# Filler of an SSD tied to single chunk outputs, and four of its sixteen tiles moved behind it

## The chip, the cores and the metric

The kernel runs on one core of a Trainium2 chip. The time is the device time of one execution in microseconds; three executions of the kernel before gave 1428.99, 1430.89 and 1433.18, median 1430.89. A profiled execution took 1432.96, with 1431.1 from its first to its last instruction; all durations below are from that one. The engines are PE (matmuls), DVE, ACT and POOL (elementwise work), and SP (which issues most DMAs).

## The reference

Two layers over 1024 tokens of width 1024 in float32, batch 1. The change touches the first layer only:

```python
def _even_layer(x, w_in, conv_w, conv_b, a_log, dt_bias, d_skip, norm_g, sc_conv_w, w_out):
    proj = x @ w_in
    z, xbc, dt_raw, sc_bg, sc_cg, sc_h, sc_gate = _split(proj, EVEN_SIZES)
    xbc = jax.nn.silu(_depthwise_conv(xbc, conv_w, SSD_CONV_PAD) + conv_b)
    xs, bm, cm = _split(xbc, (SSD_INNER, SSD_GROUPS * SSD_STATE, SSD_GROUPS * SSD_STATE))
    y_a = _ssd_bidirectional(xs, bm, cm, dt_raw, a_log, dt_bias, d_skip)   # shapes left out
    y_a = _rms_norm(y_a * jax.nn.silu(z), norm_g)
    y_b = sc_bg * _depthwise_conv(sc_cg * sc_h, sc_conv_w, (1, 1)) * jax.nn.silu(sc_gate)
    return jnp.concatenate([y_a, y_b], axis=-1) @ w_out

def _ssd_chunked(x, dt, a, bm, cm):          # one direction; 8 chunks of 128 tokens
    ...
    cb = jnp.einsum('bclgn,bcsgn->bcgls', cq, bq)
    y_diag = jnp.einsum('bcgls,bcgrls,bcsgrp->bclgrp', cb, _segsum_exp(cs), xd)
    states = jnp.einsum('bclgn,bcgrl,bclgrp->bcgrpn', bq, decay_states, xd)
    _, h_in = lax.scan(step, h0, (states, chunk_tot))   # h * exp(tot) + st, chunk by chunk
    y_off = jnp.einsum('bclgn,bcgrpn,bcgrl->bclgrp', cq, h_in, jnp.exp(cs))
    return y_diag + y_off
```

There are 16 heads of 64 in 4 groups of 4 heads; a group shares B and C (128 states). Branch B (`y_b`, the short convolution) needs four projections of 1024 columns each (sc_bg, sc_cg, sc_h, sc_gate) and nothing of the SSD.

## The kernel before

Every float32 product is made of fp32r matmuls on a high and a low part (hi·hi, hi·lo, lo·hi; `mm3` and `mm6`, L416 to L428). The list of operations is written by `main_plan` (L78) and run in that order; the framework then places the instructions in each engine's order by a simulation of its own, in which an instruction that is ready early may move ahead of others. `tc.issue_after(i)` adds an order edge: what is issued under it is not placed ahead of instruction i. It is an order, not a wait.

The first layer goes in five stages.

1. The input is split and the gate z of group 0 and dt are made. Then four tiles of branch B (j = 0).
2. Eight pairs of projections for x, B and C of the SSD. A pair is two weight tiles multiplied by a scheme of seven products in place of eight (`op_sp`, L937): 7 x 4 x 3 = 84 matmuls of 512 columns. Two separate tiles take 2 x 48.
3. The SSD, group by group. For each of eight chunks, in the order C2: three transposes (`xps`), a decay-weighted x (`xd`, split on ACT into `xdh` and on POOL into `xdl`) and the state product (`sps`) (`op_p2`, `op_p2s`); from group 1 on also the 24 gate matmuls of that chunk (`zps`, `op_z`). Then the late state additions (`op_p2b`: `hm` on POOL, an addition on DVE). Then, in the order C3, the outputs (`op_p3f` and `op_p3b`, L795 to L845): C·B into `cbp` (L801); the decay tile E, loaded by DMA from `crow` into one of four buffers (L804), biased on ACT (L809), merged under a mask on DVE (L810, L811), through Exp on ACT (L813), times C·B on DVE (L818); the state part `yo` on PE (L831), and the diagonal part on PE (L836, `cbp<-ssd,E`; "yd" in the code), which is the last to read E. Then additions on POOL and DVE, the gate, and a square on ACT.
4. Pairs of seven products for what is left of branch B.
5. The output projection and the norm, and then the second layer.

**The filler.** Branch B's tiles j = 1 to J0 - 1, four of 48 matmuls each (`gps`), are cut into 8 steps of 6 matmuls (`op_fm`, L696) and queued. FX steps are taken at the SSD's start, F2[g] at each of a group's eight chunks in its first half, F3[g] at each of its eight outputs. `op_hold` (L692) sets the instruction to which filler is tied by an order edge: the group's last transpose while its outputs are listed, nothing in between, and group 3's last yd behind the SSD. Only the first step of a tile is under the edge (L701: `hold is not None and kk == 0`); its other seven move as the placement has them. What is left in the queue stands behind the SSD. The values are F2 = (2, 0, 0, 0), F3 = (3, 3, 2, 2), J0 = 5: 16 tiles, and six pairs (j = 5 to 7) behind.

Of the kernel before, what the change touches and what calls it, by code (L numbers as in the profile page):

```python
# [18 lines left out]
P = 128  # L19
# [7 lines left out]
HD = 64  # L27
# [33 lines left out]


BR_ORDER = (1, 2, 0, 3)
F2, F3, FB, FX = (2, 0, 0, 0), (3, 3, 2, 2), 0, 8
JF, J0 = 1, 5
C2 = (0, 7, 1, 6, 2, 5, 3, 4)
C3 = (3, 4, 0, 7, 1, 6, 2, 5)
E_AT = 5
# [9 lines left out]
def main_plan():  # L78
    ops = []
# [5 lines left out]
    def pull(n):  # L85
        for _ in range(min(n, len(queue))):
            ops.append(queue.pop(0))
# [34 lines left out]
    for g in range(G):  # L122
        ops.append(("z0", g))
        pull(FB)
        for i, c in enumerate(C2):
            ops.append(("p2", g, c))
            if g > 0:
                ops.append(("z", g, c))
            pull(F2[g])
            if i > 0:  # L130
                ops.append(("p2s", g, C2[i - 1]))
        ops.append(("p2s", g, C2[-1]))
        ops.append(("p2b", g))
        if g + 1 < G:
            ops.append(("xl", g + 1))
        ops.append(("hold", g))
        ops.append(("p3f", g, C3[0]))
        for i, c in enumerate(C3):
            if i + 1 < NB:
                ops.append(("p3f", g, C3[i + 1]))  # L140
            if g == G - 1 and i == 2:
                ops.append(("tp", 0))
            if g == G - 1 and i == NB - 1:
                ops.append(("tp", 1))
            pull(F3[g])
            ops.append(("p3b", g, c))
        ops.append(("hold", None if g + 1 < G else "end"))
# [358 lines left out]
def layer0_main(k):  # L506
    nc, tc, a = k.nc, k.tc, k.a
    V, A, GP, PE = nc.vector, nc.scalar, nc.gpsimd, nc.tensor
# [126 lines left out]
    groups = [dict() for _ in range(G)]  # L635
# [53 lines left out]
    live = {}  # L689
    hold = None  # L690

    def op_hold(g):  # L692
        nonlocal hold
        hold = None if g is None else groups[-1]["yd"] if g == "end" else groups[g]["xp"]

    def op_fm(key, kk):  # L696
# [125 lines left out]
    def op_p3b(g, c):  # L822
        st = groups[g]
        M, yd = st.pop(("f", c))
        g4 = slice(4 * g, 4 * g + 4)
        blk = slice(P * c, P * c + P)
        xt = st["xtm"][:, c, :]
        yo = k.pb.tile([P, 512], F32, name="yo", tag="pb")
        cols = h_cols(c)
        d = dirs(cols)  # L830
        PE.matmul(yo[:, cols], st["xfm"][3][:, blk], st["hin"][:, c, cols], start=True, stop=True)  # L831
        to = t2("to")
        tov, yov = (t.rearrange("p (d h e) -> p d h e", d=2, h=HPG)[:, d] for t in (to, yo))
        V.tensor_tensor(out=tov, in0=yov, in1=bc_last(ecs4[:, c, d, g4], HD), op=ALU.mult)
        for h in range(HPG):
            st["yd"] = PE.matmul(yd[:, HD * h:HD * h + HD], M[:, P * h:P * h + P], xt[:, HD * h:HD * h + HD], start=True, stop=True).ins  # L836
        ta = t1("ta")
        GP.tensor_tensor(out=view(ta, HPG), in0=view(xt, HPG), in1=bc_last(st.pop(("cd", c)), HD), op=ALU.mult)
        for q in range(d.start, d.stop):
            GP.tensor_tensor(out=ta, in0=to[:, 256 * q:256 * q + 256], in1=ta, op=ALU.add)  # L840
        V.tensor_tensor(out=ta, in0=yd, in1=ta, op=ALU.add)
        yg = tp.tile([P, 256], F32, name="yg", tag="yg", bufs=3)
        V.tensor_tensor(out=yg, in0=ta, in1=st["zs"][:, c, :], op=ALU.mult)
        A.activation(out=ta, in_=yg, func=AF.Square, accum_out=k.ssq[:, c, g:g + 1])
        A.dma_start(out=k.yad[c, :, 256 * g:256 * g + 256], in_=yg)  # L845
# [794 lines left out]
```

## Time and profile before

| | |
|---|---|
| median of three executions | 1430.89 us (1428.99 to 1433.18) |
| the profiled execution, its span | 1432.96 us, 1431.1 us |
| PE busy | 1392.4 us (97%) |
| DVE, ACT, POOL busy | 936.3 (65%), 692.3 (48%), 443.5 us (31%) |
| E load from issue to landing, median | 6.3 us, 32 loads of 512 KB |
| a 512-column matmul in the filler, mean | about 400 ns from start to modelled end; they overlap |

Busy is the time in which an engine has an instruction under way, whatever its clock; an engine with a high share can be slowed all the same, and a mean over the span mixes stages. Matmuls are pipelined, so what one costs is read from the distance of starts, not from its duration. The granted clock (PEclk) is the share of full speed, with two levels, 1.2 and 2.4 GHz. A name in brackets behind a row of the timeline is what the engine had waited for, and how long.

### The profile page before, as it was taken

How to read it: one execution, taken by the hardware profiler on the slowest of the kernel's cores; microseconds unless marked ns; L12 is line 12 of the kernel's file. 1: busy time of each engine (PE TensorE's matmuls, PEld its weight loads, DVE VectorE, ACT ScalarE, POOL GpSimd, SP SyncE). 2: the span in 40 equal slices, each digit the busy share in tenths (PEclk: the TensorE clock that was granted, in tenths of full speed). 3: DMA queues.
4: the chain of work that ended last, by engine and by line, in shares of the span. 5: the costliest groups of instructions: out<-in, count | busy, mean ns of one | idle time of the engine just before them, and what ended most of it. 6: DMA issues, size and time to landing. Idle time of an engine off the chain costs nothing.

```text
span 1431.1 us, 19645 instructions
## 1 busy us (share of the span) xinstructions
PE 1392.4 (97%) x7215; PEld 1182.2 (83%) x7215; DVE 936.3 (65%) x1596; ACT 692.3 (48%) x1350; POOL 443.5 (31%) x420
## 2 busy tenths in 40 slices
PE   8999999999999899999999999999999999999997
PEld 7878888778888786788888888898888888988886
DVE  5887886466666677666575533723326888888485
ACT  5354554555565655333344332522225788888410
POOL 0031220344444454133210340611410454546210
PEclk9999999999999997999999999999999999999999
DMA  8332236634463424423258445201100000001232
GB/s 254 122 102 103 103 113 232 171 100 136 126 170 100 137 82 109 134 74 103 74 177 264 132 153 197 89 23 53 41 27 1 1 1 1 2 30 60 89 118 89
DMA packets 55520, 146.40 MB, mean 102 GB/s; under 512 B 6264, under 2 KB 11648, under 8 KB 55296
## 3 DMA queue, kind: packets, MB, share of 16 engines
q1 hardware_dynamic: 50816, 140.95, 31.7%
q10 hardware_dynamic: 4608, 4.20, 0.8%
q8 instruction: 57, 0.93, 0.3%
q14 instruction: 39, 0.32, 0.1%
HBM read 118.78 MB, written 26.35 MB: 101 GB/s over the span
## 4 chain that ended last, share of the span: by engine, by line
PE 69%; DVE 6%; DMA 3%; ACT 2%; issue 1%; POOL 0%; ACTq 0%; DVEq 0%
PE sA L953 5%; PE ops L427 4%; PE ops L425 4%; PE ops L424 4%; PE tps L1462 3%; PE fps L417 3%; PE fps L418 3%; PE fps L419 3%; PE sps L417 2%; PE sD L953 2%; PE sps L418 2%; PE sps L419 2%; PE gps L424 2%; PE gps L425 2%; PE gps L427 2%; PE o1ps L427 2%
## 5 line engine op out<-in xcount | busy, mean ns | idle before, releaser
L424 PE MATMUL gps<-x,whi 128*128 128x512 f32 x320 | 127.7, 399 | 0.3 <-ACT bru L672 0.3
L425 PE MATMUL gps<-x,whi 128*128 128x512 f32 x320 | 127.9, 400 | 0.0
L499 DVE TENSOR_TENSOR wlo<-wraw,whi 128x1024 fp32r<-128x1024 f32 x54 | 71.1, 1317 | 61.0 <-ACT whi L498 60.9
L1448 POOL TENSOR_SCALAR pt<-pt,sm 128x1024 f32<-128x1024 f32 x64 | 73.1, 1142 | 114.1 <-DVE sm L1447 63.5
L498 ACT CAST whi<-wraw 128x1024 fp32r<-128x1024 f32 x54 | 56.7, 1051 | 95.5 <-PE ops L427 38.2
L427 PE MATMUL gps<-x,wlo 128*128 128x512 f32 x320 | 102.7, 399 | 0.0
L902 POOL TENSOR_TENSOR s3t<-sraw 128x512 f32<-128x512 f32 x14 | 22.6, 1614 | 229.7 <-DMA sraw<-in_wt_dram 158.7
L499 DVE TENSOR_TENSOR PT<-tps,PT 128x512 fp32r<-128x512 f32 x128 | 84.1, 681 | 12.8 <-ACT PT L498 12.4
L1442 DVE TENSOR_REDUCE nm<-sps 128x1 f32<-128x1024 f32 x64 | 77.8, 1216 | 9.3 <-PE sps L419 9.0
L1446 ACT ACTIVATE pt<-sps,nm 128x1024 f32<-128x1024 f32 x64 | 71.8, 1122 | 17.6 <-DVE nm L1443 13.3
L1056 POOL TENSOR_TENSOR rs<-rs,neghalf 128x1 f32<-128x1 f32 x16 | 12.9, 811 | 210.7 <-DVE nm L1091 143.0
L498 ACT CAST PT<-tps 128x512 fp32r<-128x512 f32 x128 | 69.8, 588 | 16.1 <-PE tps L1462 15.6
L417 PE MATMUL fps<-x1hi,whi 128*128 128x512 f32 x192 | 74.9, 390 | 0.0
L419 PE MATMUL fps<-x1hi,wlo 128*128 128x512 f32 x192 | 74.7, 389 | 0.0
L418 PE MATMUL fps<-x1lo,whi 128*128 128x512 f32 x192 | 74.7, 389 | 0.0
L427 PEld LDWEIGHTS gps<-x,wlo 128*128 128x128 f32 x320 | 60.4, 190 | 14.0 <-issue 1.4
L424 PEld LDWEIGHTS gps<-x,whi 128*128 128x128 f32 x320 | 60.9, 190 | 13.3 <-ACT bru L672 0.8
L425 PEld LDWEIGHTS gps<-x,whi 128*128 128x128 f32 x320 | 60.9, 190 | 12.6 <-issue 0.7
L1462 PE MATMUL tps<-consts,pt 128*128 128x128 f32 x512 | 70.2, 273 | 0.3 <-DVE PT L499 0.3
L499 POOL TENSOR_TENSOR xdl<-xd,xdh 128x512 fp32r<-128x512 f32 (+1 forms) x32 | 38.8, 1213 | 101.8 <-ACT xdh L498 98.2
L646 DVE SCALAR_TENSOR_TENSOR cacc<-u,vec,cacc 128x1023 f32<-128x1023 f32 (+1 forms) x48 | 65.8, 1383 | 3.3 <-ACT cacc L643 3.0
L1477 PE MATMUL yps<-PT,vv 128*128 128x256 f32 x256 | 65.7, 286 | 0.0
(377 smaller groups left out, 4199.9 us busy)
## 6 DMA issues: line engine op xcount, KB each, us to landing
wraw<-in_wt_dram SPq DMA_DIRECT2D x70, 512.0 KB, 4.2
E<-crow SPq DMA_DIRECT2D x32, 512.0 KB, 6.3
sraw<-in_wt_dram SPq DMA_DIRECT2D x28, 512.0 KB, 3.7
xtraw<-in_xT_dram SPq DMA_DIRECT2D x16, 512.0 KB, 4.1
xbd<-cacc SPq DMA_DIRECT2D x16, 512.0 KB, 2.6
ssd<-xbd SPq DMA_DIRECT2D x16, 512.0 KB, 5.2
ybd<-bra SPq DMA_DIRECT2D x16, 256.0 KB, 2.8
yad<-yg ACTq DMA_DIRECT2D x32, 128.0 KB, 4.0
```

What stands on the lines that cost most here:

```text
L417: nc.tensor.matmul(out, shi, mhi, start=start, stop=False)
L418: nc.tensor.matmul(out, shi, mlo, start=False, stop=False)
L419: nc.tensor.matmul(out, slo, mhi, start=False, stop=stop)
L424: nc.tensor.matmul(out, shi, mhi, start=start, stop=False)
L425: nc.tensor.matmul(out, shi, mlo, start=False, stop=False)
L427: nc.tensor.matmul(out, slo, mhi, start=False, stop=stop)
L498: cast = nc.scalar.copy(out=hi, in_=src)
L499: lo_eng.tensor_tensor(out=lo, in0=src, in1=hi.bitcast(F32), op=ALU.subtract)
L953: st["last"] = PE.matmul(ps, s_[:, kk, :], x_, start=fresh and kk == 0 and m == 0, stop=kk == 3 and m == 2, skip_group_check=True).ins
L1442: V.tensor_reduce(out=nm, in_=ps, axis=AX.X, op=ALU.max)
L1448: GP.tensor_scalar(out=pt, in0=pt, scalar1=sm, scalar2=1.0, op0=ALU.mult, op1=ALU.mult)
L1462: PE.transpose(out=ps[:, P * c:P * c + P], in_=pt[:, P * (4 * h + c):P * (4 * h + c) + P], identity=k.ident)
```

## The change

```diff
-F2, F3, FB, FX = (2, 0, 0, 0), (3, 3, 2, 2), 0, 8
-JF, J0 = 1, 5
+F2, F3, FB, FX = (1, 0, 0, 0), (1, 1, 2, 3), 0, 8
+JF, J0 = 1, 4
...
                 ops.append(("tp", 1))
+            if i > 1:
+                ops.append(("hold", g, C3[i - 2]))
             pull(F3[g])
             ops.append(("p3b", g, c))
...
-    def op_hold(g):
+    def op_hold(g, c=None):
         nonlocal hold
+        if c is not None:
+            hold = groups[g]["yd", c]
+            return
         hold = None if g is None else groups[-1]["yd"] if g == "end" else groups[g]["xp"]
...
         for h in range(HPG):
-            st["yd"] = PE.matmul(yd[:, HD * h:HD * h + HD], M[:, P * h:P * h + P], xt[:, HD * h:HD * h + HD], start=True, stop=True).ins
+            st["yd"] = st["yd", c] = PE.matmul(yd[:, HD * h:HD * h + HD], M[:, P * h:P * h + P], xt[:, HD * h:HD * h + HD], start=True, stop=True).ins
```

J0 = 4 leaves 12 tiles in the filler and makes eight pairs behind the SSD. At the third and every later output of a group, filler that starts a tile is tied to the yd two outputs back. Group by group the plan takes 8 + 8, 0, 0, 0 steps in the first halves and 8, 8, 16, 24 at the outputs, where it took 8 + 16, 0, 0, 0 and 24, 24, 16, 16. The changed kernel has five lines more: its helpers' lines are two further down than before, those of the outputs five.

PE's order at the first outputs of group 0 (`yo` the state part, `cbp<-...E` the diagonal part, E_ with a number one chunk's decay tile, `gps` filler), before:

```order
L424 MATMUL gps<-x_91,whi 128x512
L836 MATMUL cbp<-ssd_1886,E_2265 128x64 x4
L425 MATMUL gps<-x_91,whi 128x512
L836 MATMUL cbp<-ssd_1886,E_2284 128x64 x4
L831 MATMUL yo<-ssd_1885,ssd_1887 128x512
L424 MATMUL gps<-x_93,whi 128x512
L425 MATMUL gps<-x_93,whi 128x512
L427 MATMUL gps<-x_91,wlo 128x512
L427 MATMUL gps<-x_93,wlo 128x512
```

And now, with the third to the fifth output (`zps` is a gate product of group 1):

```order
L421 MATMUL zps<-whi,x_93 128x256
L841 MATMUL cbp<-ssd_1886,E_2208 128x64 x4
L841 MATMUL cbp<-ssd_1886,E_2227 128x64 x4
L836 MATMUL yo<-ssd_1885,ssd_1887 128x512
L841 MATMUL cbp<-ssd_1886,E_2276 128x64 x4
L806 MATMUL cbp<-ssd_1887 128x128
L836 MATMUL yo<-ssd_1885,ssd_1887 128x256
L806 MATMUL cbp<-ssd_1887 128x128
L841 MATMUL cbp<-ssd_1886,E_2318 128x64 x4
L836 MATMUL yo<-ssd_1885,ssd_1887 128x256
L806 MATMUL cbp<-ssd_1887 128x128
```

No filler stands among the outputs of group 0 any more, nor among those of group 1; 24 gate matmuls of group 1 moved ahead of the first output and 24 behind it.

ACT's order there (`dtx` marks the Exp, `ed` the bias step, `cbp<-consts` the mask, `ta,ssq` the square), before:

```order
L813 ACTIVATE E_2345<-E_2345,dtx 128x128 x4
L809 ACTIVATE E_2469<-E_2469,ed 128x128 x4
L844 ACTIVATE ta,ssq<-yg 128x256
L845 DMA yad<-yg 128x256
L809 ACTIVATE E_2522<-E_2522,ed 128x128 x4
L498 CAST whi<-wraw 128x1024
L672 COPY bru<-gps 128x1024
L844 ACTIVATE ta,ssq<-yg 128x256
L845 DMA yad<-yg 128x256
L810 COPY cbp<-consts 128x128 x2
L813 ACTIVATE E_2399<-E_2399,dtx 128x128 x4
```

And now:

```order
L818 ACTIVATE E_2227<-E_2227,dtx 128x128 x4
L815 COPY cbp<-consts 128x128
L818 ACTIVATE E_2276<-E_2276,dtx 128x128 x4
L814 ACTIVATE E_2359<-E_2359,ed 128x128 x4
L815 COPY cbp<-consts 128x128
L814 ACTIVATE E_2400<-E_2400,ed 128x128 x4
L818 ACTIVATE E_2318<-E_2318,dtx 128x128 x4
L814 ACTIVATE E_2442<-E_2442,ed 128x128
```

Both times the Exp of the fourth chunk (E_2399, now E_2318) stands behind the bias step of the sixth (E_2522, now E_2400), whose buffer is the second chunk's; the weight cast, the filler's copy and the squares that stood between are gone from there.

PE's order at the last outputs of group 3, before:

```order
L801 MATMUL cbp<-ssd_1886 128x128
L831 MATMUL yo<-ssd_1885,ssd_1886 128x512
L836 MATMUL cbp<-ssd_1886,E_5008 128x64 x4
L801 MATMUL cbp<-ssd_1886 128x128
L831 MATMUL yo<-ssd_1885,ssd_1886 128x512
L836 MATMUL cbp<-ssd_1886,E_5068 128x64 x4
L836 MATMUL cbp<-ssd_1886,E_5125 128x64 x4
```

And now:

```order
L429 MATMUL gps<-x_93,wlo 128x512
L426 MATMUL gps<-x_91,whi 128x512
L427 MATMUL gps<-x_91,whi 128x512
L841 MATMUL cbp<-ssd_1886,E_4902 128x64
L806 MATMUL cbp<-ssd_1886 128x128
L841 MATMUL cbp<-ssd_1886,E_4902 128x64 x3
L836 MATMUL yo<-ssd_1885,ssd_1886 128x512
L426 MATMUL gps<-x_93,whi 128x512
L427 MATMUL gps<-x_93,whi 128x512
L429 MATMUL gps<-x_91,wlo 128x512
L429 MATMUL gps<-x_93,wlo 128x512
L836 MATMUL yo<-ssd_1885,ssd_1886 128x512
```

There the last five outputs stood without filler; now filler stands between outputs up to the last one.

## Rows read from the trace of the kernel before

**Rows 1.** The page: busy time, share of the span, instructions of each engine.
```profile
PE 1392.4 (97%) x7215; PEld 1182.2 (83%) x7215; DVE 936.3 (65%) x1596; ACT 692.3 (48%) x1350; POOL 443.5 (31%) x420
```

**Rows 2.** Busy time by stage: stretch, length, PE, PEld, DVE, ACT, POOL, PEclk, DMA share, GB/s.
```profile
246.50:299.50 53.00, 50.30 (x222) 40.66 (x221) 28.12 (x49) 27.71 (x69) 17.45 (x18) 0.94 0.53 149
266.00:279.00 13.00, 10.63 (x51) 8.26 (x50) 7.86 (x16) 8.34 (x24) 8.42 (x8) 0.86 0.63 147
299.50:337.20 37.70, 36.59 (x204) 29.54 (x203) 28.26 (x61) 19.81 (x61) 17.20 (x24) 1.00 0.60 164
337.20:377.80 40.60, 39.15 (x261) 35.53 (x260) 23.63 (x56) 24.81 (x74) 21.04 (x25) 1.00 0.33 99
377.80:415.40 37.60, 37.60 (x205) 30.86 (x204) 25.83 (x58) 20.45 (x63) 17.23 (x23) 1.00 0.66 168
415.40:455.80 40.40, 40.40 (x278) 37.30 (x277) 22.40 (x51) 24.66 (x72) 19.43 (x23) 1.00 0.36 106
455.80:490.50 34.70, 31.46 (x176) 25.33 (x176) 27.43 (x61) 18.74 (x61) 14.09 (x20) 0.95 0.50 143
490.50:529.50 39.00, 38.53 (x260) 35.17 (x259) 25.55 (x52) 26.83 (x75) 19.07 (x19) 1.00 0.26 80
529.50:567.00 37.50, 34.11 (x136) 25.29 (x135) 29.81 (x67) 19.38 (x62) 21.65 (x26) 0.75 0.45 116
544.00:567.00 23.00, 19.61 (x63) 13.57 (x63) 16.30 (x43) 14.95 (x49) 10.40 (x15) 0.60 0.26 80
592.20:735.00 142.80, 142.72 (x654) 118.15 (x655) 92.18 (x97) 50.85 (x66) 42.45 (x29) 0.99 0.29 94
```

**Rows 3.** Timeline of PE (start, duration, instruction) in filler; gate matmuls alone by stage.
```profile
286.51 0.39 PE L424 MATMUL gps<-x,whi 128*128 128x512 f32 x1
...
287.88 0.39 PE L424 MATMUL gps<-x,whi 128*128 128x512 f32 x1
...
474.60:477.70 3.10, 3.10 (x26) 3.10 (x26) 0.00 (x0) 0.00 (x0) 1.00 0.68 199
```

**Rows 4.** Timeline of ACT at the start of group 0.
```profile
257.51 1.01 ACT L672 COPY bru<-gps 128x1024 f32<-128x1024 f32 x1 [4.71 <-DMA xbd<-cacc]
...
261.06 0.39 ACT L498 CAST xdh<-xd 128x256 fp32r<-128x256 f32 x1
```

**Rows 5.** Timeline of PE at the first outputs of group 0.
```profile
299.53 1.02 PE L831 MATMUL yo<-ssd,ssd 128*128 128x512 f32 x2
...
303.11 1.00 PE L836 MATMUL cbp<-ssd,E 128*128 128x64 f32 x8
```

**Rows 6.** Timeline of ACT at the fourth to sixth chunk of group 0.
```profile
312.24 0.40 ACT L809 ACTIVATE E<-E,ed 128x128 f32<-128x128 f32 x1 [1.35 <-DMA E<-crow]
...
316.75 2.45 ACT L813 ACTIVATE E<-E,dtx 128x128 f32<-128x128 f32 x8 [0.61 <-DVE E L811]
```

**Rows 7.** Timeline of PE from group 2's fourth output to group 3's first transpose.
```profile
473.54 1.00 PE L836 MATMUL cbp<-ssd,E 128*128 128x64 f32 x8
...
490.45 0.49 PE L742 MATMUL xps<-consts,ssd 128*128 128x128 f32 x3
```

**Rows 8.** Timeline of ACT in the same stretch: the last chunk's bias step.
```profile
481.75 1.28 ACT L809 ACTIVATE E<-E,ed 128x128 f32<-128x128 f32 x4 [2.29 <-DMA E<-crow]
```

**Rows 9.** The page: DMA issues by line, number, KB each, median us to landing.
```profile
E<-crow SPq DMA_DIRECT2D x32, 512.0 KB, 6.3
```

**Rows 10.** The tile E in group 0 (290 to 345 us).
```profile
DMA to landing us min/median/max: 4.9/5.8/8.0
```

**Rows 11.** Timeline of PE at the end of group 3: two of its outputs' state parts.
```profile
543.10 0.70 PE L831 MATMUL yo<-ssd,ssd 128*128 128x256 f32 x2
...
563.31 2.02 PE L831 MATMUL yo<-ssd,ssd 128*128 128x512 f32 x2
```

**Rows 12.** Timeline of PE at the first outputs of group 1.
```profile
377.75 1.02 PE L831 MATMUL yo<-ssd,ssd 128*128 128x512 f32 x2
...
378.82 1.90 PE L836 MATMUL cbp<-ssd,E 128*128 128x64 f32 x16
```

## The prediction

> **What bounds the kernel now.** I read the page's busy shares first: PE is busy for 97% of the span [rows 1], so at first sight each matmul taken out is time gained. I then read busy time by stage, because a share over the whole span hides stages with another limit. There [rows 2] PE is full in the pairs behind the SSD (142.7 of 142.8 us), but in the SSD (246.5 to 567.0) it is idle for 12.4 us: 2.7, 1.1, 1.5, 0, 0, 3.2, 0.5 and 3.4 in its eight stretches, two for each group of heads (state products, then outputs). Its granted clock is 0.94, 0.95 and 0.75 in three of them; the engine ran at 1.2 in place of 2.4 GHz for a part of each, and 0.06 of 53.0, 0.05 of 34.7 and 0.25 of 37.5 us are 3.2, 1.7 and 9.4 us of work not done. So the filler hides the SSD's waits nearly everywhere, except at the end of group 3, where it ran out. Third I read what PE waits for where filler is thin: the E tiles (four buffers, eight chunks to a group). The buffer is free once a chunk's output product has read it, and must come back by DMA, pass ACT twice and DVE twice, before the chunk four further on can be multiplied.
>
> **The change part by part.** A 512-column matmul starts every 0.228 us: six from 286.51 to 287.88 [rows 3]. A filler tile is 48 of them, 11.0 us; a pair of seven products is 84, 19.2 us. The change takes four tiles out of the filler (192 matmuls, 43.8 us of PE) and puts two pairs behind the SSD (168, 38.4 us). The region of the pairs is full already, with DVE at 92 of 143 us and POOL at 42 [rows 2], which hides the pairs' weight splits and evictions, so the two pairs cost their **+38.4 us** in full. Everything then hangs on how much of the 43.8 us the SSD gives back. I counted the filler matmuls in the programs' order of PE:
>
> Group 0: 240 before (169 ahead of its first output, 71 among the outputs); 96 after, all ahead. Group 1: 144 before (55 and 89); 48 after, all ahead. Group 2: 54 and 42; 48 and 48 after. Group 3: 54 and 42; 48 and 96 after. Behind the last output, 144 both times: no change there.
>
> *Group 0, up to the first output* (53.0 us). ACT is held until 257.51 by the store of the last pair's result, whose memory the SSD's pools take over, and the first xdh comes at 261.06 [rows 4]. The change touches neither, so no state product starts before 261.5; the 48 filler matmuls that stand ahead of it fit in front, PE then waits. From there the order has six chunks with no filler between them. POOL was busy for 8.4 us over four such chunks in 266 to 279 [rows 2], 2.1 each: 12.6 us. Then come 48 filler matmuls (11.0), the last products (1.5) and 24 gate matmuls of group 1 that are now ahead of the first output; 26 of them took 3.1 us [rows 3], so 2.9 in all. That ends at 289.5, with about 1 for the last state additions at 290.5 against 299.5: **-9.0**. Bounds: with nothing to wait for after 261.5 (8 us of own products, 11.0, 2.9) 283.4, which is -16.1; at the whole 3.25 us per chunk which those four took, 296, -3.5. I take the value by POOL, since it is the engine whose work a chunk can't do without.
>
> *Group 0, the outputs* (37.7 us before), now with no filler. From the first yo to the end of the second chunk's yd it was 4.6 us (299.53 to 304.11), seven filler matmuls (1.6) among them [rows 5]; the 24 gate matmuls that stand there now make it 5.9. On ACT, the Exp of the fourth chunk stands behind the bias step of the sixth, which waits for the E tile that the second chunk's yd releases. From that release to the bias step it took 8.1 us (304.11 to 312.24) [rows 5, 6]; E loads took 4.9, 5.8 (median) and 8.0 in this group, 6.3 over all [rows 9, 10]. With 6.6 (the 6.3 and an issue), 1.28 for the bias step, half of 2.45 for the Exp and 1.7 for the product with C.B and the yd, the fourth yd ends 10.8 us later. It releases the buffer of the eighth chunk, and the row for this second turn is in group 2, whose end is bare already: fourth yd over at 474.54, bias step at 481.75, next group's first transpose at 490.45 [rows 7, 8], 15.9 us, or 15.3 with a 6.6 us load. Sum: 5.9 + 10.8 + 15.3 = 32.0, **-5.7**. With loads of 4.9 (5.2 with the issue) 29.2, -8.5; with 8.1 both times 35.0, -2.7. I take the median over all, because weight loads still stand on the same queue, though fewer.
>
> The Trainium skill (DMA: Bandwidth & Descriptors, Anatomy of one DMA) gives a transfer 2.0 us fixed and its bytes at 436 GB/s; for 512 KB I estimate 3.2 us by that, and by it each of the four turns here and in group 1 would be 3.1 us shorter, the whole change would come to -1.2 us, 1429.7, which is no change. The trace disagrees: the shortest of these E loads took 4.9 us [rows 10], and the sum stays with the rows.
>
> *Group 1.* Seven filler matmuls fewer ahead of the first output: **-1.6**, PE being full there but for 1.5 us. The outputs took 37.6 us. The first yo to the end of the second yd is 3.0 us (377.75 to 380.72) [rows 12], with nothing between them now as before; 3.0 + 10.8 + 15.3 = 29.1, **-8.5**; with the short and the long loads 26.3 and 32.1, -11.3 and -5.5. The 48 gate matmuls (5.8 us) lie inside the first turn.
>
> *Group 2.* Six matmuls move from the front to the outputs, -1.4 and +1.4. Its filler now begins behind the third output and lasts to the end, where PE idled for 3.2 us and lost 1.7 to the clock; being bare at its start instead, I take **-1** (-3 to +1).
>
> *Group 3.* In front -1.4. Among the outputs 54 more filler matmuls, 12.3 us, where PE lost 3.4 idle and 9.4 to the clock: 12.8. They fit: **-1.4** in all (-2.4 to +2.6).
>
> The SSD gives back 9.0 + 5.7 + 1.6 + 8.5 + 1 + 1.4 = 27.2 us of the 43.8; 38.4 - 27.2 = **+11.2**. The profiled execution took 1432.96 (its span is 1431.1), so 1444.2; it lies 2.1 above the median of the three runs shown, 1430.89, on whose scale this is **1442**.
>
> **The rivals.**
> *Faster: PE alone decides.* Place: the outputs of groups 0 and 1 and the front of group 0. If every E load takes the 4.9 us and the front of group 0 packs without a wait, all low ends together are 16.1 + 8.5 + 1.6 + 11.3 + 3 + 2.4 = 42.9, and the time changes by 38.4 - 42.9 = -4.5: 1426. It decides only once the SSD gives back over 42.7, that is, at these ends and nowhere short of them. For it speaks the 97% of rows 1; against it that this share counts a PE at half clock as busy, and that ACT sat waiting for E with filler still around it [rows 6, 8].
> The Trainium skill (Perfetto Trace Analysis, Identifying Performance Opportunities) has the most-contended engine set the gain. By that rule the 24 matmuls fewer would be 5.5 us less, 1425.
>
> *Slower still: both bare stretches at half clock.* At the end of group 3, when the filler was gone, PE was granted 0.60 of its clock over 23 us [rows 2], and from 543.10 to 563.31 five further chunks took 20.2 us, 4.05 each [rows 11]. Eight chunks at that pace and the start make 35.3 for group 0 and 33 for group 1, -2.4 and -4.6; with the front at -3.5 and the other terms as above the SSD gives 14.5, net +23.9: 1455. For it: a chunk's own products are 2.0 us of PE (1.07 from 377.75 to 378.82, and half of 1.90 [rows 12]) in a chunk of some 3.7. Against: group 2's bare end came back to full clock at once (0.95 over the stretch). The Trainium skill (TensorE: Matmul & The Clock Gate, HAM oscillation) says that bursts of matmuls with waits between them fall back to the lower clock over and over; by that rule it is this 1455.
>
> *No change.* Fewer weight loads share the queue with E, the loads fall to 4.9 and POOL's pace in the front to less than 2: 1.4 off each of four turns, 4 more in the front, net about +1: 1432.
>
> *The edges do nothing.* An edge sits on the first step of a tile only, and it orders, it does not wait. In groups 0 and 1 no tile starts among the outputs, so there it is without effect; in groups 2 and 3 the order shows the filler spread. Without it group 3 would end bare as before, about 10 us more; that is decided by the order already, and gets no chance of its own.
>
> **How the numbers follow.** 0.3% of the time is 4.3 us, about what can be told from no change. The forecast, +4.3 to about +20, has 0.60; both stretches at half clock 0.12; no change 0.17; PE alone 0.11. So slower 0.72, same 0.17, faster 0.11. The range is -3 to +25 around the median, 1428 to 1456: the low end leaves out only the last two microseconds of the low bounds, the high one some of the sum of the high bounds (-3.5, -2.7, -1.6, -5.5, +1, +2.6: 9.7 given back, +28.7).
>
> **What would show it.** Right: eight pairs dense behind the SSD, 38 us longer; group 0's outputs near 32 us and group 1's near 29 with PE well under nine tenths busy and a clock under 1; ACT waiting for E loads, and PE for the E product, far beyond before; group 3's outputs still about 37.5 us but at full clock; the first output of group 0 some 9 us earlier. Wrong: outputs of groups 0 and 1 in 26 us or less with PE full, which is the faster rival; E turns that take the rows' time while the SSD still gives back over 40, which would mean that my chain through ACT is not the one that binds; or a wait in the pairs' region, which I cost at none.

## The result and the profile after

The changed kernel takes 1451.77 us (median of four executions, 1448.48 to 1452.64), the kernel before 1432.04 (four executions, 1428.99 to 1433.65). The ratio is 1.0131, 95% interval [1.011, 1.0152]: slower, by 19.7 us. The forecast was 1442, its range 1428 to 1456. All readings below are from the profiled execution, which took 1452.45.

The busy shares on the page of the kernel after, beside [rows 1]:

```profile
PE 1391.2 (96%) x7191; PEld 1179.2 (81%) x7191; DVE 947.4 (65%) x1608; ACT 697.4 (48%) x1359; POOL 449.8 (31%) x427
```

PE has 24 matmuls and 1.2 us of busy time less, yet the span is 19.6 us longer. The page's total hides it; the stages show it. Busy time by stage after, in the columns of [rows 2]: front and outputs of groups 0 to 3, and the pairs behind the SSD:

```profile
250.50:293.70 43.20, 37.58 (x173) 30.32 (x172) 22.53 (x42) 24.50 (x62) 14.83 (x17) 0.88 0.58 163
293.70:328.10 34.40, 24.28 (x110) 17.25 (x109) 23.23 (x59) 17.59 (x63) 15.83 (x23) 0.77 0.55 139
328.10:366.10 38.00, 37.86 (x253) 34.69 (x252) 23.15 (x53) 23.51 (x72) 19.07 (x23) 0.98 0.38 111
366.10:399.60 33.50, 24.78 (x134) 18.97 (x134) 22.28 (x54) 18.24 (x61) 16.04 (x22) 0.82 0.75 148
399.60:437.90 38.30, 37.94 (x253) 34.84 (x252) 22.96 (x52) 23.35 (x72) 18.82 (x24) 0.98 0.39 119
437.90:470.00 32.10, 31.12 (x181) 25.28 (x181) 24.68 (x56) 20.50 (x63) 12.95 (x19) 1.00 0.67 154
470.00:510.00 40.00, 37.68 (x254) 34.19 (x253) 26.34 (x55) 24.76 (x71) 21.52 (x21) 1.00 0.28 76
510.00:549.20 39.20, 37.65 (x190) 29.54 (x189) 32.82 (x71) 21.68 (x68) 21.59 (x26) 1.00 0.45 127
574.70:755.00 180.30, 180.30 (x819) 149.31 (x820) 114.42 (x119) 63.35 (x84) 55.91 (x38) 0.99 0.28 89
```

The outputs of groups 0 and 1 (second and fourth line) are the new hole: PE is busy for 24.28 of 34.4 us and 24.78 of 33.5, at a granted clock of 0.77 and 0.82. The pairs are full to the last tenth. By stage, in us:

| stage | before | forecast | after |
|---|---|---|---|
| start to the first transpose | 246.5 | 246.5 | 250.6 |
| group 0, front | 53.0 | 44.0 | 43.2 |
| group 0, outputs | 37.7 | 32.0 | 34.4 |
| group 1, front | 40.5 | 38.9 | 38.0 |
| group 1, outputs | 37.6 | 29.1 | 33.4 |
| group 2, both | 75.1 | 74.1 | 70.5 |
| group 3, both | 76.5 | 75.1 | 79.2 |
| pairs, with the transposes for the projection among them | 142.5 | 180.9 | 180.4 |

The SSD gave back 320.4 - 298.7 = 21.7 us where the forecast had 27.2. Why the outputs are long is read from the timeline of ACT in the kernel after, group 0 (L814 is the bias step, L818 the Exp; brackets: waited for, and how long):

```profile
298.24 1.28 ACT L818 ACTIVATE E<-E,dtx 128x128 f32<-128x128 f32 x4 [2.94 <-DVE E L816]
304.03 1.28 ACT L814 ACTIVATE E<-E,ed 128x128 f32<-128x128 f32 x4 [4.51 <-DMA E<-crow]
305.21 0.25 ACT L815 COPY cbp<-consts 128x128 f32<-128x128 f32 x1
307.14 1.29 ACT L814 ACTIVATE E<-E,ed 128x128 f32<-128x128 f32 x4 [1.68 <-DMA E<-crow]
308.34 1.26 ACT L818 ACTIVATE E<-E,dtx 128x128 f32<-128x128 f32 x4
...
317.90 0.69 ACT L814 ACTIVATE E<-E,ed 128x128 f32<-128x128 f32 x2 [3.36 <-DMA E<-crow]
...
319.08 1.26 ACT L818 ACTIVATE E<-E,dtx 128x128 f32<-128x128 f32 x4
```

In ACT's order these are the Exp of the third chunk, the bias step of the fifth, the mask copy of the fourth, the bias step of the sixth, the Exp of the fourth, the bias step of the eighth, and the Exp of the sixth. The fourth chunk's Exp needs nothing that the sixth has, but stands behind it, and the sixth waits for its load. In the same way the sixth's Exp stands behind the eighth's bias step. PE in the same stretch (L836 yo, L841 the diagonal product, L747 the next group's transposes):

```profile
293.74 1.02 PE L836 MATMUL yo<-ssd,ssd 128*128 128x512 f32 x2
...
297.70 1.89 PE L841 MATMUL cbp<-ssd,E 128*128 128x64 f32 x16
...
306.79 1.22 PE L836 MATMUL yo<-ssd,ssd 128*128 128x256 f32 x2 [4.37 <-DVE ta L846]
...
310.38 1.97 PE L841 MATMUL cbp<-ssd,E 128*128 128x64 f32 x8 [1.94 <-DVE E L823]
...
328.15 0.85 PE L747 MATMUL xps<-consts,ssd 128*128 128x128 f32 x3
```

The second chunk's product ends at 299.59, the fourth's at 312.35, the next group begins at 328.15: a start of 5.85 us, a first turn of 12.76, a second of 15.80. The 4.37 us at 306.79 are put down to DVE, since yo waits for a PSUM tile that DVE has to read; DVE's own timeline shows what it was held by:

```profile
305.50 0.72 DVE L816 COPY_PREDICATED E<-cbp,E 128x512 f32<-128x512 int32 x1 [3.91 <-ACT cbp L815]
```

This is the merge of the fourth chunk. It waited for ACT's mask copy (L815), which stands behind the bias step at 304.03. So this wait leads through ACT to the E load as well, but to the fifth chunk's: the merge ended at 306.22, and of the fourth Exp's delay the sixth chunk's bias step added the 2.1 us from there to 308.34. On the page of the kernel after the loads have hardly changed from [rows 9]:

```profile
E<-crow SPq DMA_DIRECT2D x32, 512.0 KB, 6.1
```

### The profile page after: what moved, and what is told of

Read it like the earlier page. It is cut to its first block, busy times and chain, and to the rows that moved or that the text cites. A ratio compares the mean times of both kernels' runs of the same rounds, so it can differ in the third digit from the quotient of the medians.

```text
span 1450.7 us, 19639 instructions
## 1 busy us (share of the span) xinstructions
PE 1391.2 (96%) x7191; PEld 1179.2 (81%) x7191; DVE 947.4 (65%) x1608; ACT 697.4 (48%) x1359; POOL 449.8 (31%) x427
## 4 chain that ended last, share of the span: by engine, by line
PE 81%; DVE 8%; DMA 6%; ACT 2%; issue 2%; POOL 1%; SPq 0%; DVEq 0%; ACTq 0%; POOLq 0%
PE sA L958 12%; PE sD L958 6%; PE ops L427 4%; PE ops L429 4%; PE ops L426 4%; PE tps L1467 3%; PE fps L421 3%; PE fps L419 3%; PE fps L420 3%; PE sB L958 3%; PE sps L419 2%; DMA E<-crow 2%; PE sps L420 2%; PE sps L421 2%; PE o1ps L427 2%; PE o1ps L429 2%
## 5 line engine op out<-in xcount | busy, mean ns | idle before, releaser
L501 DVE TENSOR_TENSOR wlo<-wraw,whi 128x1024 fp32r<-128x1024 f32 x50 | 66.9, 1338 | 56.3 <-ACT whi L500 56.2
L426 PE MATMUL gps<-x,whi 128*128 128x512 f32 x256 | 101.4, 396 | 0.0
L427 PE MATMUL gps<-x,whi 128*128 128x512 f32 x256 | 101.3, 396 | 0.0
L500 ACT CAST whi<-wraw 128x1024 fp32r<-128x1024 f32 x50 | 52.5, 1050 | 97.1 <-PE ops L429 41.6
L429 PE MATMUL gps<-x,wlo 128*128 128x512 f32 x256 | 80.8, 393 | 0.0
L500 ACT CAST whi<-sraw 128x1024 fp32r<-128x1024 f32 x40 | 41.4, 1051 | 69.4 <-PE sD L958 39.9
L1467 PEld LDWEIGHTS tps<-consts,pt 128*128 128x128 f32 x512 | 59.7, 141 | 7.2 <-DVE PT L501 1.2
L958 PE MATMUL sA<-x,whi 128*128 128x512 f32 x192 | 60.5, 396 | 3.5 <-ACT whi L500 3.5
```

The costliest lines, as they stand in the source:

```text
L426: nc.tensor.matmul(out, shi, mhi, start=start, stop=False)
L427: nc.tensor.matmul(out, shi, mlo, start=False, stop=False)
L429: nc.tensor.matmul(out, slo, mhi, start=False, stop=stop)
L500: cast = nc.scalar.copy(out=hi, in_=src)
L501: lo_eng.tensor_tensor(out=lo, in0=src, in1=hi.bitcast(F32), op=ALU.subtract)
L958: st["last"] = PE.matmul(ps, s_[:, kk, :], x_, start=fresh and kk == 0 and m == 0, stop=kk == 3 and m == 2, skip_group_check=True).ins
```

## The experiments

Theory 1 was the forecast's mechanism: what bounds bare outputs is the E tile's way back through ACT's order. Against it stood the clock, the work of DVE and POOL, and the edges as such. The kernel before was timed beside each set: 1433.55 for the first four, 1432.88 for the next four, 1432.25 for the three after and 1429.89 for the last.

**The edges alone.** The changed kernel with the old numbers:

```diff
-F2, F3, FB, FX = (1, 0, 0, 0), (1, 1, 2, 3), 0, 8
-JF, J0 = 1, 4
+F2, F3, FB, FX = (2, 0, 0, 0), (3, 3, 2, 2), 0, 8
+JF, J0 = 1, 5
```

> The changed kernel with the numbers of the kernel before (F2 = (2,0,0,0), F3 = (3,3,2,2), J0 = 5): 16 filler tiles, six pairs behind the SSD, and the new order edges. Theory 1 (bare outputs are held by the E tile's turn through ACT; what filler stands late in a group hides it): the filler of groups 2 and 3 now reaches to their last outputs, where the kernel before lost 3.2 + 1.7 and 3.4 + 9.4 us idle or at half clock; some of the 17.7 comes back late in the group and some is lost at its bare start: 1425 us (1419 to 1431), group 3's outputs at 30 to 35 us in place of 37.5 with a clock of 0.9 or more. Rival (the edges decide nothing, only the number of tiles does): 1432, the same as before, within 3 us.

Measured: 1446.3 us, ratio 1.0096 [1.0079, 1.0112]. Both expectations missed: with the old numbers the edges cost 13 us. Group 0's outputs took 48.4 us in place of 37.7 (front 46.4 in place of 53.0), group 3's 43.3 in place of 37.5. In sum group 0 lost 4.1 us (not traced) and group 3 5.2. Group 3's outputs by stage, rows of ACT there in the kernel before, and then of ACT, PE and DVE in this kernel:

```profile
535.40:578.70 43.30, 32.90 (x142) 24.70 (x141) 29.64 (x70) 22.27 (x69) 20.86 (x26) 0.76 0.39 101
```

```profile
536.24 1.28 ACT L813 ACTIVATE E<-E,dtx 128x128 f32<-128x128 f32 x4 [1.39 <-DVE E L811]
...
540.51 1.28 ACT L809 ACTIVATE E<-E,ed 128x128 f32<-128x128 f32 x4 [3.00 <-DMA E<-crow]
```

```profile
549.82 0.98 ACT L814 ACTIVATE E<-E,ed 128x128 f32<-128x128 f32 x3 [3.36 <-DMA E<-crow]
...
551.00 1.26 ACT L818 ACTIVATE E<-E,dtx 128x128 f32<-128x128 f32 x4
```

```profile
553.04 1.97 PE L841 MATMUL cbp<-ssd,E 128*128 128x64 f32 x8 [5.33 <-DVE E L823]
```

```profile
551.05 0.69 DVE L876 TENSOR_TENSOR xtraw<-xtraw 128x512 f32<-128x512 f32 x1 [2.95 <-DMA xtraw<-in_xT_dram]
552.30 0.69 DVE L823 TENSOR_TENSOR E<-E,cbp 128x512 f32<-128x512 f32 x1 [0.56 <-ACT E L818]
```

The edge ties a tile to the product two outputs back, which keeps filler away from group 3's first outputs, and the placement on ACT followed: the bias steps of the fifth and sixth chunk (the latter waits for its load at 549.82) now stand ahead of the third chunk's Exp at 551.00, where in the kernel before that Exp came ahead of both. The third product waits 5.33 us, with no filler ahead of it, at half clock. It is the same kind of order on ACT as in the changed kernel. But it is not alone here: DVE, which has to multiply that tile with C·B (L823), stood until 551.05 behind a load of the second layer's input (`xtraw`) and then waited 0.56 us more for the Exp. How the 13 us divide between the two orders was not tested. I had counted the bare start as harmless and the filled end as gain.

**The numbers alone.** The changed kernel without the edges:

```diff
-            if i > 1:
-                ops.append(("hold", g, C3[i - 2]))
```

> The changed kernel without its new order edges: 12 filler tiles, eight pairs, F2 and F3 as changed. Theory 1: group 3's filler is taken early again and its last outputs are bare, so it loses about what the kernel before lost there (12.8 us) on top of the changed kernel's 1452, less what the better filled start gives back: 1459 us (1454 to 1466). Rival (the edges decide nothing): 1452, the same as the changed kernel, within 3 us.

Measured: 1450.77, ratio 1.0115 [1.0098, 1.0132]: the rival's 1452. With these numbers the edges decide nothing in sum. Group by group they do move time: the outputs took 33.2, 31.0, 36.4 and 40.1 us without them, 34.4, 33.4, 32.1 and 39.2 with them. Group 3 did not end bare without the edges, though I had claimed that it would: its clock was 0.97; F3 = 3 puts half as much filler again there as the kernel before had.

**ACT in order.** The changed kernel and one edge on ACT; `ex` is a list for each group:

```diff
+            with tc.issue_after(ex[-2]) if len(ex) > 1 else nullcontext():
                 for h in range(HPG):
                     A.activation(out=E4[:, 1, h], ..., func=AF.Identity, ...)
...
         for h in range(HPG):
-            A.activation(out=E[:, h], ..., func=AF.Exp, ...)
+            last = A.activation(out=E[:, h], ..., func=AF.Exp, ...)
+        ex.append(last.ins)
```

> The changed kernel with one more order edge on ACT: the bias step of a chunk's E tile is not placed ahead of the Exp of the chunk two before it, so that the Exp of the fourth chunk no longer stands behind a bias step that waits for the sixth chunk's load. Nothing else is changed. Theory 1: the two turns in a row that held groups 0 and 1 become one turn and a half; their outputs fall from 34.4 and 33.4 us to about 27 each: 1439 us (1430 to 1445). Rival A (the bare stretches are long because TensorE's clock is at 1.2 GHz there, whatever ACT does): 1452 within 3. Rival B (each chunk's own work on DVE and POOL sets the pace, 28 us of DVE in a group's outputs): 30 to 33 us for each group, 1446 to 1450.

Measured: 1437.03 (twelve executions, 1435.0 to 1438.37), ratio 1.0025 [1.0014, 1.0035]; 14.7 us less than the changed kernel. The outputs of groups 0 and 1, by stage:

```profile
292.20:318.70 26.50, 20.23 (x102) 14.42 (x101) 20.62 (x53) 17.75 (x64) 14.49 (x21) 0.87 0.62 141
357.80:385.40 27.60, 22.64 (x135) 17.99 (x133) 21.26 (x51) 17.32 (x58) 15.18 (x19) 0.94 0.71 162
```

26.5 and 27.6 us against 34.4 and 33.4, with the same program but for this order: the order of two kinds of instructions on ACT was worth 13.7 us of the two stretches. A little of it only moved: one product of group 0 now stands behind its stretch, and the front of group 1 takes 1.1 us more. Rivals A and B are out as the main cause. ACT in this kernel, fifth chunk's bias step and fourth chunk's Exp, then the sixth's Exp and the eighth's bias step:

```profile
302.57 1.27 ACT L816 ACTIVATE E<-E,ed 128x128 f32<-128x128 f32 x4 [4.42 <-DMA E<-crow]
...
304.80 0.99 ACT L820 ACTIVATE E<-E,dtx 128x128 f32<-128x128 f32 x3 [0.80 <-DVE E L818]
...
312.54 1.26 ACT L820 ACTIVATE E<-E,dtx 128x128 f32<-128x128 f32 x4
...
314.45 0.40 ACT L816 ACTIVATE E<-E,ed 128x128 f32<-128x128 f32 x1 [0.49 <-DMA E<-crow]
```

The fourth's Exp comes at 304.80 in place of 308.34, but still behind one waiting bias step, since the edge reaches two chunks back. The sixth's comes at 312.54, now ahead of the eighth's bias step. From the second product's end to the fourth's it was 10.1 us in place of 12.8, from there to the next group 9.8 in place of 15.8: most of group 0's gain lies in the second turn, which the forecast took whole from group 2's row. An edge to the chunk just before was not tried.

**Three buffers.**

```diff
-T1B, T4B, T2B, CVB, RAWB, E2B = 5, 1, 5, 2, 3, 4
+T1B, T4B, T2B, CVB, RAWB, E2B = 5, 1, 5, 2, 3, 3
```

> The changed kernel with three buffers for the E tile in place of four. Theory 1: the turn comes after three chunks, so the bare outputs of groups 0 and 1 need about one turn more (some 13 us at most, some 5 at least, each), groups 2 and 3 with filler less: 1468 us (1458 to 1482). Rivals (clock, or DVE and POOL set the pace): 1452 within 4.

Measured: 1446.93 (1445.68 to 1456.22), ratio 1.0111 [1.0084, 1.0137]: a clear miss, 5 us under the changed kernel and not 16 over it. In the profiled execution, the slowest of the four, the two outputs took 35.5 and 34.0 us. ACT shows why (fifth chunk's bias step, then the fourth's Exp):

```profile
306.24 1.27 ACT L814 ACTIVATE E<-E,ed 128x128 f32<-128x128 f32 x4 [2.04 <-DMA E<-crow]
307.42 1.26 ACT L818 ACTIVATE E<-E,dtx 128x128 f32<-128x128 f32 x4
```

The Exp of the fourth chunk comes at 307.42, behind the load into the second chunk's buffer, just as with four (308.34). In the changed kernel the fourth buffer is thus worth nothing: its chunk has its data early and queues on ACT. I had counted turns as if each buffer shortened them. If so, three buffers must cost time once ACT is in order; that was the next test of it.

**Three buffers and ACT in order.** Both edits.

> The changed kernel with three E buffers and the ACT edge. Theory 1, as it stands now: in the changed kernel the Exp of the fourth chunk stands behind the bias step of the sixth and so behind the load into the second chunk's buffer, which makes the fourth buffer worthless, and three buffers cost nothing. With the Exp in its place the number of buffers counts again: three buffers lose most of what the ACT edge gave with four, outputs of groups 0 and 1 at 32 us or more, 1446 us (1441 to 1451). Rival (the edge helps by another way than the buffers, such as by bringing the first Exp forward): 1437 within 3, as with four.

Measured: 1450.21, ratio 1.0128 [1.0112, 1.0145], 13.2 over the run with four. The outputs of groups 0 and 1:

```profile
291.80:319.80 28.00, 24.03 (x103) 17.19 (x102) 22.03 (x51) 16.28 (x57) 15.56 (x21) 0.72 0.57 139
363.80:396.50 32.70, 27.89 (x136) 21.36 (x135) 21.74 (x50) 17.99 (x60) 17.05 (x21) 0.79 0.57 148
```

They took 28.0 and 32.7 us (26.5 and 27.6 with four), and the fronts of groups 1 and 2 44.0 and 42.2 (39.1 and 37.9), where the late products of the last chunks now stand. The buffers count once ACT is in order, as expected; that half of it would show in the next fronts, with group 0 under the 32 that I named, was not.

**PE kept busy for nothing.** The changed kernel with idle matmuls in groups 0 and 1:

```diff
+        for _ in range(8 if g < 2 else 0):
+            PE.matmul(yd, st["xfm"][3][:, blk], st["hin"][:, c, cols][:, 0:256], start=True, stop=True)
         for h in range(HPG):
             st["yd"] = st["yd", c] = PE.matmul(...)
```

> The changed kernel with 8 matmuls of 256 columns more in each output of groups 0 and 1, between yo and the diagonal product, into the place that the diagonal product then overwrites: 128 matmuls of 0.12 us at full clock, some 15 us of PE, that compute nothing. Theory 1 (PE waits there for ACT and E): they lie in the waits, 1451 us (1447 to 1457), with the granted clock of the two groups' outputs at 0.95 or more in place of 0.77 and 0.82; what the full clock gives back is only the late diagonal products, 1.0 us in place of 2.0 each, one or two to a group on the chain. Rival A (the half clock makes the stretches long): the outputs get shorter by the 7.9 and 6.0 us of clock lost there, as far as the added work allows: 1440 to 1446. Rival B (PE is full there in effect): 1466.

Measured: 1474.0, ratio 1.0299 [1.0281, 1.0317]. The price of the added work was wrong: they ran as f32, two records of 0.215 us each, not as one of 0.12. The state parts and the diagonal products are f32 too, two records for each matmul in the rows; so not every float32 product of this kernel is split into fp32r matmuls. PE's timeline at an output of group 0 and at the group's end (L841 the added matmuls, L747 the next group's transposes), and the whole of group 0's outputs:

```profile
302.81 3.62 PE L841 MATMUL cbp<-ssd,ssd 128*128 128x256 f32 x16
306.26 1.00 PE L843 MATMUL cbp<-ssd,E 128*128 128x64 f32 x8
...
334.30 0.49 PE L747 MATMUL xps<-consts,ssd 128*128 128x128 f32 x3
334.63 0.60 PE L841 MATMUL cbp<-ssd,ssd 128*128 128x256 f32 x2
...
293.60:334.30 40.70, 40.70 (x222) 34.78 (x222) 24.82 (x61) 18.11 (x63) 15.35 (x23) 1.00 0.42 121
```

It is 3.45 us for each output (302.81 to 306.26). Seven of the eight lie in the stretch, 24.2 us; the eighth output's stand behind the next group's first transpose. The stretch grew by 6.3, from 34.4 to 40.7, with PE full at a clock of 1.00. So 17.9 of the 24.2 lay in waits and half clock, and the stretch's own work is 40.7 - 24.2 = 16.5 us at full clock. The totals of the three theories don't apply to this added work. What it shows: of the 34.4 us in the changed kernel 16.5 are work, PE is idle for 10.1 (34.40 - 24.28), and the other 7.8 are about what half clock adds. It does not tell which of the two comes first, since the added work takes away both.

**ACT in order, in the kernel before.**

> The kernel before (its filler numbers, no new filler edges) with the ACT edge alone: a chunk's bias step not ahead of the Exp of the chunk two before it. Theory 1 (the hoisted bias steps hold the outputs wherever filler does not cover them): only the bare ends of groups 2 and 3 can gain, which lost 3.2 + 1.7 and 3.4 + 9.4 us; about half of that: 1424 us (1417 to 1430). Rival (filler covers the ACT waits before, the ends are bound by their own work): 1432 within 3.

Measured: 1426.14, ratio 0.9957 [0.9942, 0.9972]: the kernel before lost 6 us to the same order on ACT. Group 2's outputs fell from 34.6 to 32.3 us and group 3's from 37.5 to 35.9; 2.5 came in group 0's front and 1.6 in group 1's, which the expectation did not have. Group 3's end is still bare, at a clock of 0.81:

```profile
524.20:560.10 35.90, 31.87 (x136) 23.47 (x135) 29.33 (x64) 19.18 (x63) 20.30 (x26) 0.81 0.50 112
```

**The filler's place, with ACT in order.** The changed kernel's numbers, the filler edges taken out and the ACT edge put in (the two diffs above):

> The changed kernel's filler numbers (12 tiles, eight pairs) without its filler edges, with the ACT edge. Theory 1: groups 0 and 1 as in the run with both edges (26.5 and 27.6 us of outputs); groups 2 and 3 have their filler early, with ends that are bare but no longer held by ACT: 1437 us (1433 to 1442), so with 12 tiles the filler edges decide nothing. Rival (with ACT in order the filler edges are worth their spreading): 1443 or more, over the 1437 of the run with both.

Measured: 1437.94, ratio 1.0041 [1.0027, 1.0054]; with the filler edges it was 1437.03. They are worth nothing here either.

The kernel before with the ACT edge and a more even filler:

```diff
-F2, F3, FB, FX = (2, 0, 0, 0), (3, 3, 2, 2), 0, 8
+F2, F3, FB, FX = (1, 0, 0, 0), (3, 3, 3, 3), 0, 8
```

> 16 filler tiles, six pairs, no filler edges, the ACT edge, and the filler more even: F2 = (1,0,0,0), F3 = (3,3,3,3), so that group 3 has 144 filler matmuls at its outputs where the kernel before had 108. Theory 1: ACT does not hold the outputs and filler stands in nearly every group to its end; of the 12.4 us idle and 14.3 us lost to the clock in the SSD of the kernel before, 12 to 20 come back: 1416 us (1410 to 1424). Rival (PE-bound but with the loss moved elsewhere, as with the edges alone): 1430 or more.

Measured: 1421.51 (1417.83 to 1423.2), ratio 0.9923 [0.9906, 0.9939]: faster than both kernels, the best of all. Its outputs of groups 0 to 3, by stage:

```profile
295.00:330.20 35.20, 35.20 (x197) 29.06 (x196) 26.82 (x59) 21.19 (x67) 17.22 (x24) 1.00 0.62 186
...
368.10:406.80 38.70, 38.70 (x206) 31.57 (x205) 30.32 (x64) 22.09 (x65) 16.81 (x21) 1.00 0.62 153
...
446.40:484.90 38.50, 38.50 (x204) 31.40 (x203) 28.09 (x61) 21.69 (x64) 14.76 (x20) 1.00 0.62 144
...
526.50:568.20 41.70, 37.08 (x184) 29.31 (x183) 34.26 (x69) 22.89 (x67) 21.74 (x26) 0.97 0.47 110
```

PE is full at full clock in three of the four; what was a hole of 10 us in the changed kernel holds filler here. The same numbers with the filler edges as well:

> The same as the run before it, but with the new filler edges as well. Theory 1: the edges keep filler out of the first outputs of a group and put it late, so that the first outputs are bare: 3 to 8 us above the run without them, 1422 us (1415 to 1430). Rival (spread over single outputs, filler hides more): at or below the run without the edges.

Measured: 1422.51, ratio 0.9928 [0.991, 0.9947]: the same as without the edges, the rival. What the edges cost with the old numbers (13 us) they don't cost here, where ACT is in order; that the order is the reason is not shown, since the numbers differ too. The kernel before with the ACT edge and filler added to groups 2 and 3 alone:

```diff
-F2, F3, FB, FX = (2, 0, 0, 0), (3, 3, 2, 2), 0, 8
+F2, F3, FB, FX = (2, 0, 0, 0), (3, 3, 3, 3), 0, 8
```

> 16 filler tiles, six pairs, no filler edges, the ACT edge, F2 = (2,0,0,0), F3 = (3,3,3,3): the fuller front of group 0 that the kernel before had, and group 3's outputs filled to their end. Theory 1: the kernel before with the ACT edge (1426) still had 20.4 us at half clock at the end of group 3 or next to it; filling that gives back about 5: 1421 us (1416 to 1425). Rival (the eight filler steps that stood behind the SSD only move): 1426 within 2.

Measured: 1426.26, ratio 0.9957 [0.9942, 0.9972]: the rival (its eight steps are sixteen by the numbers: eight more in each of groups 2 and 3). More filler for these two alone brought nothing over 1426.14; taking eight steps from group 0's front is what 1421.51 has besides. The changed kernel without filler edges, with the ACT edge, and with one step more at each output of groups 0 and 1:

```diff
-F2, F3, FB, FX = (1, 0, 0, 0), (1, 1, 2, 3), 0, 8
+F2, F3, FB, FX = (1, 0, 0, 0), (2, 2, 2, 3), 0, 8
```

> 12 filler tiles and eight pairs as in the changed kernel, no filler edges, the ACT edge, F3 = (2,2,2,3) in place of (1,1,2,3), so that some filler also stands among the first outputs of groups 0 and 1. Theory 1: the first outputs are not held by E, so filler there covers little; the later ones stay bare: 1436 us (1431 to 1441), over the 1421 of 16 tiles by what four tiles and their cover are worth. Rival (it is the distribution and not the number of tiles): 1425 or less.

Measured: 1435.24, ratio 1.0019 [1.0005, 1.0032], as expected: with ACT in order, no placement of twelve tiles that was tried comes near sixteen.

## Why the prediction held, and where it was off

**The pairs: held.** +38.4 forecast; 142.5 to 180.4 us is +37.9, with PE busy for 180.30 of 180.3.

**The mechanism in groups 0 and 1: held, shown.** The forecast's chain (release, load, bias step, Exp of the fourth chunk behind the sixth's bias step) stands row for row in ACT's timeline above, and undoing this kind of order on ACT gave back 13.7 us there. Two links were missing from it: the fourth's mask copy behind the fifth's bias step, and in the second turn the sixth's Exp behind the eighth's. The order is also not the whole loss: with the ACT edge in both kernels the change still costs some 10 us (1426.14 to 1437.03, ratios 0.9957 and 1.0025) in place of 19.7. So about half of the loss goes through this order, and the other half is what the two pairs cost beyond what the SSD gives back even with ACT in order. The rival by PE alone is out: [rows 1]'s 97% fell to 96% while the time rose.

**Its size: off in group 0 by 2.4, in group 1 by 4.3 us.** Start 5.85 for the 5.9 forecast; first turn 12.76 for 10.8; second 15.80 for 15.3. Of the first turn's 2.0 too little, 0.95 are the load (299.59 to the bias step at 307.14, 7.55 for the 6.6 that I took) and 1.0 is the last product at half clock (1.97 us for 1.0 in [rows 5]). In the second the load was quicker (312.35 to 317.90, 5.55) and the rest slower (10.25 for 8.7 in [rows 7, 8]), with two yo and a product at half clock, 1.8 to 2.1 us each. In group 1 the start was 3.0, as forecast, and the 4.3 are two misses that cancel in part: the first turn took 18.7 us for 10.8 (second product over at 369.11, fourth at 387.83), the second 11.8 for 15.3.

```profile
379.39 0.40 ACT L814 ACTIVATE E<-E,ed 128x128 f32<-128x128 f32 x1 [2.51 <-DMA E<-crow]
...
392.79 0.69 ACT L814 ACTIVATE E<-E,ed 128x128 f32<-128x128 f32 x2 [2.75 <-DMA E<-crow]
```

```profile
386.19 1.65 PE L841 MATMUL cbp<-ssd,E 128*128 128x64 f32 x8
...
399.58 0.85 PE L747 MATMUL xps<-consts,ssd 128*128 128x128 f32 x3
```

In the first turn the sixth chunk's bias step came 10.3 us after the release, for the 6.6 taken; the fourth's merge and Exp came 1.0 later than counted; and its product was over 4.9 us after its Exp, for 1.7, behind a yo at half clock. The E loads issued in this stretch took 4.8 to 10.1 us, median 7.4. I took the median of all loads for every turn. But the first turn starts with two buffers that come free within the 1.89 us of the two products, and it is the slower of two loads that holds ACT (7.6 and 10.3 us from release to bias step); in the second turn ACT waits for a single load (5.6 and 5.0).

The Trainium skill (DMA: Bandwidth & Descriptors, Anatomy of one DMA), by whose figures I estimated 3.2 us for such a load, gives them there for DMAs issued by POOL (GpSimd), and E is issued by SP [rows 9]. The trace after does not agree with them either: no load of groups 0 and 1 took under 4.6 us.

**The rival by the clock: half of it is there.** Its 35.3 and 33 us for the two stretches lie nearer to the measured 34.4 and 33.4 than the forecast's 32.0 and 29.1. Its premise did not hold: the granted clock was 0.77 and 0.82, half clock for 15.7 of the 34.4 us and 12.1 of the 33.4, not throughout. And the time came back by an order on ACT, with the clock rising (0.87 and 0.94) as the waits went: of the 13.7 us some 7.5 were idle time of PE, and some 6.2 busy time, of which 1.0 is the product that moved and the rest goes with the higher clock. The Trainium skill (TensorE: Matmul & The Clock Gate, HAM oscillation) describes bursts between waits that fall to the lower clock; the trace agrees on the clock, with half-clock stretches of 10.2 and 6.8 us in group 0's outputs and twice 6.8 in group 1's, but in these runs the half clock shrank when the order on ACT was undone, so it comes with the waits here and adds to them. How long the stretches would be at full clock with the old order, no run shows.

**Fronts: held in size.** Group 0 -9.8 for the -9.0 by POOL's pace, group 1 -2.5 for -1.6. The six bare chunks took 12.1 us (265.42 to 277.51) for the 12.6, but PE's waits among them end with ACT's xdh, 1.12, 1.00 and 0.24 us, and only 0.17 with POOL; that POOL sets the pace is not shown. The slow bound of this term was also mis-added: its parts come to 296.4, or 297.4 with the microsecond for the state additions, so -3.1 or -2.1 in place of -3.5.

```profile
268.15 0.58 PE L419 MATMUL sps<-xdh,bhl 128*128 128x256 f32 x1 [1.12 <-ACT xdh L500]
...
270.82 0.80 PE L419 MATMUL sps<-xdh,bhl 128*128 128x512 f32 x1 [1.00 <-ACT xdh L500]
```

**Group 2 and group 3: wrong in sign or size.** Group 2 gave 4.6 us in place of 1: the bare start that I charged for cost 1.0 us of waits (31.12 of 32.1 busy), since the first outputs have their E tiles early, and the end that idled for 3.2 us is filled. Group 3 lost 2.7 where I had it gain 1.4. Its outputs did run at full clock with the 54 more matmuls (37.65 busy of 39.2), as forecast, but 1.7 us longer; and its front idled for 2.3 us, where it had been 0.5, at the transition from group 2.

**The edges: misjudged.** I said that the order decides about 10 us in group 3 in their favour. Taken out, they changed nothing (1450.77); put alone into the kernel before, they cost 13 us. I read in PE's order where the filler stands, and not in ACT's and DVE's what the edges moved there.

**4.1 us ahead of the SSD: open.** Up to the first transpose the order of every engine is the same in both kernels. The stretch took 246.5 us in the profiled execution before, 250.6 after, and 247.5 to 250.7 in the twelve others, three of which (248.4, 248.3 and 247.5) keep the kernel before's numbers of tiles and of steps in group 0's front. The execution before is the shortest of the fourteen: PE's wait for a copy on ACT in the pairs there (`snap`) took 0.3 us in it and 1.3 to 2.7 in the thirteen others. I take it for spread of single executions, which one profile each can't show.

Together: -0.5 in the pairs, +5.5 in the SSD and +4.1 ahead of it, over the forecast's +11.2, make some 20 us; the spans differ by 19.6. That the SSD came out only 5.5 us off is in part luck: its terms missed by -0.8 and +2.4 in group 0, -0.9, +7.9 and -3.6 in group 1, -3.6 in group 2 and +4.1 in group 3.

## What to carry to other kernels

Filler hides waits; before it is taken out, look for the order that makes the wait, because the wait may be free to remove while the filler is not. An instruction that waits for a load, placed by a scheduler ahead of one that is ready, makes a buffer worthless: if one buffer fewer costs nothing, look at the order of the engine that uses it. And a duration with a wide spread does not go into a chain by one median: a step that waits for two loads in order gets the slower of them.

## What the runs showed of the hardware

The loads of E, 512 KB each, all of one form, took 4.6 to 13.4 us within one execution of the changed kernel, median 6.1. A product of two f32 operands of 256 columns took two records of 0.215 us on PE at full clock, 0.43, against 0.12 for the fp32r gate matmul of the same width. The granted clock returned to 1.00 and stayed there for 40.7 us, the whole of group 0's outputs, once the waits between outputs were filled with matmuls, whatever these compute.
